# A hybrid attention block on one core: one store on another queue, one early load, two left forms behind a residual sum, and left forms taken by quarter

## The chip, the cores and the metric

The kernel runs on one core of a Trainium2 chip. Its time is the device time of one execution in microseconds (us); the figure of a kernel is the median of its runs. Beside the times there is one profiled execution, whose trace gives the start and the duration of nearly every instruction on TensorE (PE, with its weight loads as PEld), VectorE (DVE), ScalarE (ACT), GpSimd (POOL) and on SyncE's queue (SP), which issues most of the DMAs.

## The reference, cut to what matters

One layer on x of 512 rows by 2048 columns, float32:

```python
h  = rmsnorm(x, g_attn)
qa, ka, va, qb, kb, vb, f = split(h @ w_in)        # 8 + 8 heads of 128, and 8 gate columns
oa = stick_breaking_attention(qa, ka, va)          # 8 heads
ob = forgetting_attention(qb, kb, vb, cumsum(log_sigmoid(f + b_f)))   # 8 heads
x  = x + concat(headnorm(oa), headnorm(ob)) @ w_out        # w_out: 2048 x 2048
x  = x + relu(rmsnorm(x, g_mlp) @ w_up)**2 @ w_down        # 2048 x 8192, 8192 x 2048
y  = rmsnorm(x, g_final)
```

## The kernel before, in words

**Products.** Every float32 operand is split into a high part (a cast to fp32r on ACT) and a low part (what is left, a subtraction on DVE): `split`, L56 to L65. A product is three matmuls, high by high, high by low and low by high (`mm3`, L77 to L80). In a trace the three are lines L78, L79 and L80; a matmul of 128x128 by 128x512 that follows another without a wait starts 0.227 us after it. A weight tile is thus loaded as float32 by a DMA (`wraw`, `wo`, `wu`, `wd`), cast (`wh`, or `wx` where a second pair of rooms is used) and subtracted (`wl`).

**Stages.** First comes the gate and value part of the input projection, whose scaled results (`s`, scaled by the row's 1/rms) are stored to a DRAM buffer `vd` (`added`, L585 to L590: two DVE operations, then the DMA). Then follow 16 periods of 26 us, one for each head: the projections of q and k (`accq`), scores (`s`), the attention weights, and their product with v (`o`). What happens when within a period is a table of times: each job is put into a plan with `plan.at(time, job)`, and the plan is sorted by time and written out in that order (class `Plan`). In parallel the weights of the output projection are read, summed and split, and the results stored to DRAM (`wsums`, `whigh`, `wraws`). In the last period, in place of a projection, the first part of the output projection is multiplied into `acc` (class `Second`): four weight pieces of 2 x 128 rows, in the order m0 = 4, 6, 0, 2, whose high and low parts come ready from `wraws` (`load_parts`, L1142 to L1146, two DMAs each: `wh` and `wl`, for m0 = 2 both are called `w` and take rooms that held the input's left operand). At about the same time the queue issues the transposing DMA (L945, `pl<-pt`) that turns the attention weights of a head.

**The output stage** (L1490 on) computes the rest of the residual sum by a scheme of seven products instead of eight (forms p = 1 to 7; form 2 is what class `Second` multiplies; the others come in the order 1 and 4, 5, 6, 3, 7 for column half db = 0 and 1, 5, 6, 3, 7, 4 for db = 1). `g_form` makes the left operand of a form out of `mixed` (the head outputs), with at most one DVE sum or difference (`a_source`, L1335 to L1341) and a `split` (ACT cast, DVE subtraction). `out_piece(p, db, m0)` loads a weight piece and multiplies it into one of three accumulators in PSUM (`accoa`, `accob`, `accoc`). `take(p, db)` adds an accumulator to a quarter of x (DVE, L1552). When a quarter is complete, `turn_quarter` transposes it on PE in two groups of four (`tr`, L1559), ACT scales it into `hr` (L1565), SP stores it (L1574) and ACT sums its squares (L1586). Out of `hr`, `left_form` makes the seven left operands `f` of the MLP's first product, again with `a_source` and `split`. For db = 0 the quarter (0,0) is taken after the last piece of form 1, and its transposes stand after the first piece of form 5; the left operands of forms 3 and 7 are made piece by piece beside the pieces of forms 5 and 6, released by `last_heads[4]`, which is the last low part made before (L1622). `pending` lists left forms that wait for their turn in the second half.

All engines have hand-written orders: a scheduler places each instruction behind the one named in `tc.issue_after`, and each engine then runs its own list strictly in order. An instruction that waits therefore holds all that stands behind it on its engine, and this is so for SP's queue of DMAs too.

Of the kernel before, what the change touches and what calls it, by code (L numbers as in the profile page):

```python
# [12 lines left out]
ALU = mybir.AluOpType  # L13
# [25 lines left out]
def block_kernel(ctx, tc, x, g_attn, w_in, b_f, g_out_sb, g_out_fox, w_out, g_mlp, w_up, w_down, g_final, y):  # L39
    nc = tc.nc  # L40
    pe, act, dve, pool, sp = nc.tensor, nc.scalar, nc.vector, nc.gpsimd, nc.sync
# [14 lines left out]
    lows, last_heads = [None], [None] * 7  # L56
# [65 lines left out]
    vd = [dp.tile([P, TB, 2 * P], F32, name="vd0")] + [dp.tile([P, TB, 2 * NVS[i]], F32, name=f"vd{i}") for i in (1, 2)]  # L122
# [99 lines left out]
    with ExitStack() as stage:  # L222
# [23 lines left out]
        plan = Plan()  # L246
# [68 lines left out]
        t0, step = 5.9, 1.93  # L315
# [13 lines left out]
        for k in range(2, K8):  # L329
            if k < 6:  # L330
                room[k] = early_w[0][:, 4:6] if k == 2 else early_w[1][:, 2 * k - 6:2 * k - 4]
                w = Placed(room[k])
            else:
                w = Piece(w_rows[k][:, :, c0:c0 + m], 2, m)
# [41 lines left out]
        for k in range(4, K8):  # L376
            t, j = mm_at[k], k + K8
            w = pieces[k][0]
# [206 lines left out]
        def added(name, T, t0, group, j):  # L585
            out = keep[name]
            for i in range(2):
                dve.scalar_tensor_tensor(out[:, i, :], T[0][:, i, :out.shape[2]], r1s[0][:, t0 + i:t0 + i + 1], out[:, i, :], op0=ALU.mult, op1=ALU.add)
            n = NVS[group]
            sp.dma_start(vd[group][:, t0:t0 + 2, j * n:(j + 1) * n], out)  # L590

        r1s = [None]
        gate = {}
# [172 lines left out]
    with tc.tile_pool(name="att", bufs=1, side="right", reuse_waits="tile") as at, \  # L766
# [9 lines left out]
        plan = Plan()  # L776
# [403 lines left out]
        for n in range(2 * NH + 1):  # L1180
            t = TPER * n
            i_s, i_o = n - 1, n - 2
            if n < 2 * NH:
                pieces = []
                for a, (which, hf) in enumerate(((0, 0), (0, 1), (1, 0), (1, 1))):
                    if n == 0:
                        if a == 3:
                            plan.at(t + 16.3, first_pieces[a].cast)
                            plan.at(t + 18.2, first_pieces[a].low)
                        pieces.append(first_pieces[a])  # L1190
                        continue
                    load = (-21.0, -15.0, -14.0, -2.0)[a]
                    if n == 1:
                        cast, low = ((-7.0, -5.0), (-3.0, -2.0), (2.9, 3.9), (8.5, 9.5))[a]
                        load = (-23.0, -19.0, -13.1, -7.5)[a]
                    else:
                        cast, low = ((-12.35, -10.95), (2.3, 3.3), (3.9, 5.2), (9.7, 11.2))[a] if n <= NH else ((-9.25, -3.65), (2.3, 3.3), (3.3, 4.5), (13.6, 15.1))[a]
                        if a == 0 and n == NH + 1:
                            cast, low = -12.35, -10.95
                    w = q_piece(n, which, hf)  # L1200
                    if a == 3 and n > 2:
                        plan.at(t - 0.5, load_behind, w)
                        load = None
                    pieces.append(w.plan(plan, load and t + load, t + cast, t + low))
                marks = [(0, 0, 8, 0.0), (1, 0, 8, 7.35), (2, 0, 8, 14.8), (3, 0, 4, 20.3), (3, 4, 8, 23.4)]
                if n == 0:
                    marks = [(2, 0, 2, 16.2), (2, 2, 8, 17.6), (3, 0, 4, 21.6), (3, 4, 8, 24.3)]
                for a, k0, k1, dt in marks:
                    plan.at(t + dt, project, n, (0, 0, 1, 1)[a], pieces[a], a % 2, k0, k1)
                late = n <= NH  # L1210
                for which, times in ((0, (19.0, 19.75, 20.45) if n == 0 else (14.4, 18.9, 19.9) if late else (12.8, 17.9, 23.6)),
                                     (1, (TPER + 1.0, TPER + 1.7, TPER + 2.4))):
                    for dt, f in zip(times, (scale_u, high_u, low_u)):
                        plan.at(t + dt, f, n, which)
            else:
                for i, jobs in ((1, (-9.25, -3.65)), (0, (2.3, 3.3))):
                    for dt, f in zip(jobs, (fox_left.high, fox_left.low)):
                        plan.at(t + dt, f, i)
                unit = 0
                for db in range(2):  # L1220
                    for n0, m0 in enumerate((4, 6, 0, 2)):
                        w = Second(db, m0)
                        if db:
                            plan.at(t + (-10.0, -9.0, -8.0, 6.0)[n0], w.load)
                            plan.at(t + (3.4, 4.5, 10.3, 11.35)[n0], w.cast_apart if n0 < 2 else w.cast, *((n0,) if n0 < 2 else ()))
                            plan.at(t + (4.6, 7.0, 11.75, 12.95)[n0], w.low)
                        else:
                            plan.at(t + (-11.0, -5.5, 0.1, 0.2)[n0], w.load_parts)
                        for tt in range(2):
                            plan.at(t + at_unit16(unit), w.multiply, tt)  # L1230
                            unit += 1
                for db in range(2):
                    plan.at(t + 2.0 + db, load_second_x, db)
                    for tt in range(2):
                        plan.at(t + (20.6, 28.5)[db] + 0.75 * tt, take_second, db, tt)
                t_end = t + at_unit16(15) + 1.37
# [31 lines left out]
        t = TPER * 2 * NH  # L1268
# [229 lines left out]
    def g_form(p, *parts):  # L1498
        for m0, m1 in parts:
            a_form(p, mixed_halves[:, m0:m1], [g[:, m0:m1, :] for g in G[p]])  # L1500
# [35 lines left out]
            begun_ = sp.dma_start(raw, wsums[:, m0 // 2, {5: 0, 7: 1, 4: 2, 6: 3}[p], db])  # L1536
        return raw, begun_

    units, casts = [], [None]
    first_loads = [(u, k, slice(a, a + 2)) for u in range(2) for k in range(2) for a in range(0, KC // 2, 2)]  # L1540
    hr, quarter = [[None, None], [None, None]], {}

# [4 lines left out]
    def take(p, db):  # L1547
        qs, ps = {1: ([(0, 0)], chains[db]), 5: ([(1, 1)], C), 6: ([(0, 1)], chains[db]),
                  7: ([(1, 1), (1, 0)], chains[db]), 3: ([(0, 1)], C), 4: ([(1, 0)], (early_4, C)[db])}[p]
        for q in qs:  # L1550
            for t in range(2) if p == 4 else [slice(0, 2)]:
                dve.tensor_tensor(quarter[q][:, t, :], quarter[q][:, t, :], ps[:, t, :], op=ALU.add)  # L1552

    def turn_group(t0, j, db, a):
        x_ = quarter[t0, j]
# [35 lines left out]
        a_form(p, hr[db][j], [F[p][db][:, 2 * j:2 * j + 2, c, :] for c in range(2)])  # L1591

    pending, to_turn = [], []
    for db in range(2):
        quarter[0, 0] = second_x[db]
        if db == 1:
            pending += [(1, 0, j) for j in (1, 0)]
        else:

            g_form(1, (0, 4), (4, 6))  # L1600
            with tc.issue_after(last_heads[2].ins):
                g_form(4, (0, 4), (4, 8))
            with tc.issue_after(last_heads[5].ins):
                g_form(5, (0, 4), (4, 6))
            more_parts.append(lambda: parts_at(px, "px"))
            with tc.issue_after(last_heads[3].ins):
                out_piece(1, 0, 0)
            with tc.issue_after(last_heads[0].ins):
                out_piece(1, 0, 2)
                out_piece(1, 0, 4)  # L1610
            begin(1, 0, 0)
            with tc.issue_after(last_heads[1].ins):
                for m0 in (0, 2, 4, 6):
                    ins = out_piece(4, 0, m0)
            for p in (1, 5):
                g_form(p, (6, 7), (7, 8))
            take(4, 0)
            with tc.issue_after(ins.ins):
                begin(1, 1, 0)
            with tc.issue_after(last_heads[6].ins):  # L1620
                g_form(6, (0, 4), (4, 6), (6, 8))
            last_heads[4] = lows[0]  # L1622
        for p in (1, 5, 6, 3, 7, 4)[:6 if db else 5]:
            for m0 in (6,) if db == 0 and p == 1 else (0, 2, 4, 6):
                ins = out_piece(p, db, m0)
                if m0 in (0, 2) and to_turn:
                    with tc.issue_after(ins.ins):
# [16 lines left out]
                if db == 0 and p == 5 and m0 == 6:  # L1644

                    with tc.issue_after(ins.ins):
                        begin(0, 1, db)
                if db == 0 and p in (6, 5) and m0 != 0:

                    with tc.issue_after(last_heads[4].ins):  # L1650
                        g_form({5: 3, 6: 7}[p], {2: (0, 4), 4: (4, 6), 6: (6, 8)}[m0])
            if db == 0 and p == 6:
                more_parts.pop()
                px_cm.__exit__(None, None, None)
# [5 lines left out]
                begin(1, 1, db)  # L1660
            if db == 1 and p == 3:
                begin(1, 0, db)
            take(p, db)
            if db == 1:
                pending += [(q, 0, j) for q in {1: (4, 5, 6), 6: (2, 7, 3)}.get(p, ()) for j in range(2)]
            if len(squares) > 0:

                with ExitStack() as order_:
                    if casts[0] is not None:
                        order_.enter_context(tc.issue_after(casts[0].ins))  # L1670
                    take_squares()
            to_turn += [q + (db,) for q in {1: [(0, 0)], 3: [(0, 1)], 7: [(1, 1)] if db else [(1, 1), (1, 0)]}.get(p, ())]
            if db == 1 and p == 6:
                left_form(1, 1, 0)
        if db == 1:
# [167 lines left out]
    plan, groups = Plan(), {}  # L1843
# [9 lines left out]
    for u, p, begin_, total, cast, low in (  # L1853
# [3 lines left out]
        w = FirstProduct(u, p)  # L1857
# [4 lines left out]
    for p, j, total, cast, low in ((7, 1, None, -1.0, 1.5), (4, 0, None, 5.95, 7.1), (5, 0, 7.8, 8.45, 9.7), (6, 0, 14.1, 14.85, 16.0),  # L1862
                                   (7, 0, 16.7, 17.45, 18.6), (3, 1, 24.2, 25.5, 26.35), (3, 0, 27.0, 28.4, 28.5)):
        w = Left(p, j)
# [85 lines left out]
    with tc.manual_schedule(engines={pe.engine, act.engine, dve.engine}):  # L1950
# [7 lines left out]
        for k in range(len(steps)):  # L1958
            n = steps[k][2]
# [6 lines left out]
            w, p = at_step(k - 1)  # L1966
# [298 lines left out]
```

## Time and profile before

| what | value |
|---|---|
| median of 3 runs | 2015.63 us (2014.76 to 2016.26) |
| the profiled execution | 2014.26 us |
| its span, first to last instruction | 2012.5 us |
| granted TensorE clock, mean over the span | 0.998 |
| PE busy | 1992.4 us (99%) |
| DVE busy | 1754.9 us (87%) |
| ACT busy | 1205.4 us (60%) |
| data moved by DMA | 426.66 MB, 212 GB/s on average |

The profiled execution is 1.37 us faster than the median, and 1.8 us of it lie outside the span. Views of the trace give, for an instruction or a run of equal ones, the start in us from the span's start, the duration, the engine and line, the operation with its output and inputs, and in brackets the idle time of the engine just before it and what ended that. A list of waits adds such idle times up by what was waited for. Lines are those of the kernel before.

### The profile page before, as it was taken

The page shows a single profiled execution, that of the slowest core. Times are in us where ns is not written, and L with a number is a line of the kernel's source. Part 1 is how long each engine was busy: PE and PEld are TensorE (multiplying, and loading weights), DVE is VectorE, ACT ScalarE, POOL GpSimd, SP SyncE. Part 2 cuts the span into 40 slices and gives each one's busy share as a digit, 9 for nine tenths or more (in the row PEclk, how much of TensorE's full clock was granted, in tenths as well). Part 3 has the DMA queues.
Part 4 walks back from the last instruction along what each step waited for, and adds up shares of the span by engine and source line. Part 5 has one row for each costly group of instructions (what it writes and reads, how often), then busy time and mean ns, then how long its engine had stood idle before and what let it go on. Part 6 is the DMA issues. An engine that isn't in the chain of part 4 may idle for free.

```text
span 2012.5 us, 26673 instructions
## 1 busy us (share of the span) xinstructions
PE 1992.4 (99%) x10096; PEld 1710.1 (85%) x10096; DVE 1754.9 (87%) x1992; ACT 1205.4 (60%) x1636; POOL 64.8 (3%) x73
## 2 busy tenths in 40 slices
PE   9999999999999999999999999999999999999998
PEld 9988788888887889888888888888888888888887
DVE  7876788888888579999999999998798888888896
ACT  7543567778875466776676767766543444444444
POOL 0000011101110000000000000000000000000003
PEclk9999999999999999999999999999999999999999
DMA  7335877677797872566666675666794674674642
GB/s 259 126 141 178 285 252 233 200 226 216 225 286 249 261 259 99 166 209 214 201 197 204 197 223 187 206 203 233 251 330 175 228 269 162 232 266 167 217 164 84
DMA packets 309072, 426.66 MB, mean 212 GB/s; under 512 B 49440, under 2 KB 198736, under 8 KB 302416
## 3 DMA queue, kind: packets, MB, share of 16 engines
q1 hardware_dynamic: 308192, 422.85, 63.5%
q10 hardware_dynamic: 752, 2.11, 0.3%
q8 instruction: 79, 1.29, 0.2%
q14 instruction: 49, 0.40, 0.1%
HBM read 318.07 MB, written 97.01 MB: 206 GB/s over the span
## 4 chain that ended last, share of the span: by engine, by line
PE 95%; DMA 2%; DVE 2%; ACT 1%; issue 0%; SPq 0%; DVEq 0%; ACTq 0%
PE psa L1415 11%; PE accd L80 8%; PE accd L78 8%; PE accd L79 8%; PE psa L1413 6%; PE psc L1415 5%; PE accq L78 5%; PE accq L79 5%; PE accq L80 5%; PE psc L1413 3%; PE psb L1415 3%; PE psb L1413 1%; PE m L80 1%; PE m L79 1%; PE m L78 1%; PE vy L78 1%
## 5 line engine op out<-in xcount | busy, mean ns | idle before, releaser
L2051 ACT CAST wh<-wd 128x1024 fp32r<-128x1024 f32 x126 | 125.0, 998 | 167.4 <-PE accd L80 55.9
L1937 DVE TENSOR_TENSOR wl<-wu,wh 128x1024 fp32r<-128x1024 f32 x157 | 191.4, 1220 | 13.4 <-ACT wh L1931 13.4
L80 PE MATMUL accq<-hH,wl 128*128 128x512 f32 x512 | 199.5, 390 | 1.1 <-DVE wl L180 1.1
L78 PE MATMUL accq<-hH,wh 128*128 128x512 f32 x512 | 200.4, 391 | 0.0
L79 PE MATMUL accq<-hL,wh 128*128 128x512 f32 x512 | 199.4, 389 | 0.0
L1931 ACT CAST wh<-wu 128x1024 fp32r<-128x1024 f32 x157 | 166.4, 1060 | 48.5 <-PE psc L1415 22.9
L1415 PE MATMUL psa<-f,wh 128*128 128x512 f32 x712 | 177.1, 391 | 0.0
L79 PE MATMUL accd<-wl,uf 128*128 128x512 f32 x436 | 169.6, 389 | 0.0
L80 PE MATMUL accd<-wh,uf 128*128 128x512 f32 x436 | 169.6, 389 | 0.0
L78 PE MATMUL accd<-wh,uf 128*128 128x512 f32 x436 | 169.4, 389 | 0.0
L2058 DVE TENSOR_TENSOR wl<-wd,wh 128x1024 fp32r<-128x1024 f32 x126 | 144.0, 1152 | 11.5 <-ACT wh L2051 11.5
L1415 PEld LDWEIGHTS psa<-f,wh 128*128 128x128 f32 x712 | 130.8, 188 | 25.3
L2051 ACT CAST wx<-wd 128x1024 fp32r<-128x1024 f32 (+1 forms) x82 | 80.8, 995 | 107.9 <-PE accd L80 43.2
L1772 DVE TENSOR_TENSOR m<-m,accd 128x1024 f32<-128x1024 f32 x84 | 102.3, 1217 | 48.5 <-PE accd L80 48.5
L80 PEld LDWEIGHTS accq<-hH,wl 128*128 128x128 f32 x512 | 96.1, 188 | 21.9 <-DVE wl L180 1.6
L79 PEld LDWEIGHTS accq<-hL,wh 128*128 128x128 f32 x512 | 96.2, 188 | 18.9
L78 PEld LDWEIGHTS accq<-hH,wh 128*128 128x128 f32 x512 | 96.2, 188 | 18.9
L78 PE MATMUL accd<-wx,uf 128*128 128x512 f32 x284 | 110.5, 389 | 0.0
L79 PE MATMUL accd<-wx,uf 128*128 128x512 f32 x284 | 110.5, 389 | 0.0
L80 PE MATMUL accd<-wx,uf 128*128 128x512 f32 x284 | 110.5, 389 | 0.0
L1413 PEld LDWEIGHTS psa<-f,wl 128*128 128x128 f32 x712 | 94.8, 191 | 5.2
L1413 PE MATMUL psa<-f,wl 128*128 128x256 f32 x712 | 97.2, 282 | 0.0
(498 smaller groups left out, 5073.8 us busy)
## 6 DMA issues: line engine op xcount, KB each, us to landing
wu<-in_w_up_dram SPq DMA_DIRECT2D x60, 1024.0 KB, 6.6
ufd<-st SPq DMA_DIRECT2D x98, 512.0 KB, 3.6
wd<-in_w_down_dram SPq DMA_DIRECT2D x48, 1024.0 KB, 8.4
uf<-ufd SPq DMA_DIRECT2D x42, 1024.0 KB, 7.0
wraw<-in_w_in_dram SPq DMA_DIRECT2D x64, 512.0 KB, 5.8
wo<-wsums SPq DMA_DIRECT2D x28, 512.0 KB, 5.3
wd<-in_w_down_dram SPq DMA_DIRECT2D x16, 768.0 KB, 8.3
uf<-ufd SPq DMA_DIRECT2D x14, 768.0 KB, 4.5
```

Of the source, the lines that this page charges most:

```text
L78: pe.matmul(out, sh, mh, start=first, stop=False, skip_group_check=True)
L79: pe.matmul(out, sh, ml, start=False, stop=False, skip_group_check=True)
L80: return pe.matmul(out, sl, mh, start=False, stop=last, skip_group_check=True)
L1413: ins = pe.matmul(ps[:, 2 * P:], lo[:, a, :], f_parts(p, a)[0], start=False, stop=last, skip_group_check=True)
L1415: ins = pe.matmul(ps, hi[:, a, :], f_both(p, a), start=a == PAIRS[0] and p in (1, 5), stop=last, skip_group_check=True)
L1772: dve.tensor_tensor(M[p][:, :, db, :], M[p][:, :, db, :], ps, op=ALU.add)
L1931: act.copy(rooms[k][0], srcs[k])
L1937: lows[0] = dve.tensor_tensor(lo, srcs.pop(k), hi.bitcast(F32), op=ALU.subtract)
L2051: act.copy(rooms[k + 3][0], srcs[k + 3])
L2058: dve.tensor_tensor(rooms[k + 2][1], srcs.pop(k + 2), rooms[k + 2][0].bitcast(F32), op=ALU.subtract)
```

## The change

Six places change.

1. The last store of scaled values (group 2, name "21") is issued by ACT's queue, the others stay on SP's.
2. The parts of the piece m0 = 2, the fourth of `Second`, are loaded by the plan at t - 1.4 instead of t + 0.2; the transposing DMA of the head before stands at t - 1.25 and the piece m0 = 0 at t + 0.1.
3. The left operands of forms 3 and 7 are made later: a table `G_AT` says beside which piece (p, m0) which parts are made, and they are released by the residual sum of quarter (0,0) (`taken[0]`), not by the last low part before.
4. For db = 0 the last piece of form 1, the sum of quarter (0,0) (`take(1, 0)`) and the entry of its transposes into `to_turn` move from ahead of form 5 to ahead of form 5's last piece; the transposes come after the first piece of form 6.
5. With that, `take` and `to_turn` skip form 1 of db = 0 at their old place.
6. In `pending`, left forms of db = 1 are listed quarter by quarter (j outer, form q inner) instead of form by form.

```diff
@@ added
-            sp.dma_start(vd[group][:, t0:t0 + 2, j * n:(j + 1) * n], out)
+            (act if group == 2 and name == "21" else sp).dma_start(vd[group][:, t0:t0 + 2, j * n:(j + 1) * n], out)
@@ the plan of the last period
-                            plan.at(t + (-11.0, -5.5, 0.1, 0.2)[n0], w.load_parts)
+                            plan.at(t + (-11.0, -5.5, 0.1, -1.4)[n0], w.load_parts)
@@ take
-                dve.tensor_tensor(quarter[q][:, t, :], quarter[q][:, t, :], ps[:, t, :], op=ALU.add)
+                taken[0] = dve.tensor_tensor(quarter[q][:, t, :], quarter[q][:, t, :], ps[:, t, :], op=ALU.add)
@@ output stage
+    G_AT = {(5, 6): (3, (0, 4), (4, 6)), (6, 0): (3, (6, 8)), (6, 2): (7, (0, 4)), (6, 4): (7, (4, 6)), (6, 6): (7, (6, 8))}
...
-            last_heads[4] = lows[0]
         for p in (1, 5, 6, 3, 7, 4)[:6 if db else 5]:
-            for m0 in (6,) if db == 0 and p == 1 else (0, 2, 4, 6):
+            for m0 in () if db == 0 and p == 1 else (0, 2, 4, 6):
+                if db == 0 and p == 5 and m0 == 6:
+                    out_piece(1, 0, 6)
+                    take(1, 0)
+                    last_heads[4] = taken[0]
+                    to_turn += [(0, 0, 0)]
                 ins = out_piece(p, db, m0)
...
-                if db == 0 and p in (6, 5) and m0 != 0:
+                if db == 0 and (p, m0) in G_AT:
 
                     with tc.issue_after(last_heads[4].ins):
-                        g_form({5: 3, 6: 7}[p], {2: (0, 4), 4: (4, 6), 6: (6, 8)}[m0])
+                        g_form(*G_AT[p, m0])
...
-            take(p, db)
+            if db == 1 or p != 1:
+                take(p, db)
             if db == 1:
-                pending += [(q, 0, j) for q in {1: (4, 5, 6), 6: (2, 7, 3)}.get(p, ()) for j in range(2)]
+                pending += [(q, 0, j) for j in range(2) for q in {1: (4, 5, 6), 6: (2, 7, 3)}.get(p, ())]
...
-            to_turn += [q + (db,) for q in {1: [(0, 0)], 3: [(0, 1)], 7: [(1, 1)] if db else [(1, 1), (1, 0)]}.get(p, ())]
+            to_turn += [q + (db,) for q in {1: [(0, 0)] if db else [], 3: [(0, 1)], 7: [(1, 1)] if db else [(1, 1), (1, 0)]}.get(p, ())]
```

The first place is the end of the value part (about 175 to 195 us of the trace). ACT's order there, with - for rows of before alone and + for rows of the changed kernel alone; `wh<-wraw` are casts of projection weights of the first head, `vd` is the DRAM buffer of values:

```order
 L173 CAST wh<-q_1573 128x1024
 L173 CAST wh<-r_1593 128x1024
-L173 CAST wh<-wraw 128x1024 x3
+L173 CAST wh<-wraw 128x1024 x2
+L590 DMA vd_89<-s_1700 128x2x512
+L173 CAST wh<-wraw 128x1024
 L801 CAST uh<-qf 128x512
 L173 CAST wh<-wraw 128x1024
```

The store stands between the second and the third cast; on SP's queue its row is gone from between a load of `wraw` and the load of `rb` (L784), and nothing else moves there.

The second place is SP's queue at the start of the last period (about 581 to 596 us). `wh` and `wl` are the parts of the pieces m0 = 6 and then m0 = 0, `w` with a number those of the piece m0 = 2, and the transposing DMA is that of the head before:

```order
 L1146 DMA wh<-wraws_94 128x1024
 L1146 DMA wl<-wraws_94 128x1024
+L1146 DMA w_5249<-wraws_94 128x1024
+L1146 DMA w_5248<-wraws_94 128x1024
 L1146 DMA wh<-wraws_94 128x1024
+L945 DMA_TRANSPOSE pl<-pt 128x20x128
 L1146 DMA wl<-wraws_94 128x1024
-L1146 DMA w_5264<-wraws_94 128x1024
-L945 DMA_TRANSPOSE pl<-pt 128x20x128
-L1146 DMA w_5265<-wraws_94 128x1024
 L166 DMA wraw<-in_w_out_dram 128x2x512
 L1536 DMA wo<-wsums 128x1024
```

Both parts of m0 = 2 now stand ahead of the transposing DMA, and the low part of m0 = 0 stands behind it, where before the second part of m0 = 2 stood. Three loads are ahead of the transposing DMA in both orders.

The third place is DVE's order around the sum of quarter (0,0) (about 646 to 663 us). The rows L1341 and L1339 are the differences for the left operands of forms 3 and 7, `g` their low parts, `x<-x,accoa` the sum of quarter (0,0), and `x<-x,accoc` that of form 5's quarter:

```order
 L61 TENSOR_TENSOR g_5518<-mixed,g_5517 128x512
+L1552 TENSOR_TENSOR x_5278<-x_5278,accoa 128x1024
 L1341 TENSOR_TENSOR mixed<-mixed 128x4x256
 L1341 TENSOR_TENSOR mixed<-mixed 128x2x256 x2
 L1339 TENSOR_TENSOR mixed<-mixed 128x4x256
 L1339 TENSOR_TENSOR mixed<-mixed 128x2x256 x2
-L1552 TENSOR_TENSOR x_5278<-x_5278,accoa 128x1024
-L61 TENSOR_TENSOR wx<-wo,wx 128x1024
+L1552 TENSOR_TENSOR x_5703<-x_5703,accoc 128x1024
 L61 TENSOR_TENSOR g_5522<-mixed,g_5521 128x1024
```

The sum of quarter (0,0) moves ahead of the six differences, and the low part of a weight piece (`wx`) leaves its place behind it, since that piece is loaded earlier. On PE the transposes `tr` of this quarter move from ahead of the first piece of form 6 to behind it. In the second half of the stage the two transpose groups of one quarter, which stood 12 matmuls apart, now stand one right behind the other, and on DVE the difference `hr` for a left operand of form 7 (L1339) now stands ahead of a weight's low part (`wl<-wu,wh`, L1838) instead of behind it.

More of the change, by code (lines that the diff above doesn't have):

```diff
@@ L1537, in out_weights @@
         return raw, begun_
-    units, casts = [], [None]
+    units, casts, taken = [], [None], [None]
     first_loads = [(u, k, slice(a, a + 2)) for u in range(2) for k in range(2) for a in range(0, KC // 2, 2)]
```

## The prediction

> **What bounds the kernel now.** I read the page first, then PE's list of waits, then the timeline around each wait. The page's row for PE (busy us, share of the span, instructions):
>
> ```profile
> PE 1992.4 (99%) x10096; PEld 1710.1 (85%) x10096; DVE 1754.9 (87%) x1992; ACT 1205.4 (60%) x1636; POOL 64.8 (3%) x73
> ```
>
> PE is busy for 1992.4 of 2012.5 us, and the change alters no matmul, only orders. So all that it can take away is idle PE time, and all that it can cost is new idle time. PE's waits (us in total, times, longest):
>
> ```profile
> PE tr L1559 <- DVE x L1552: 4.3, 1, 4.3
> PE acc L79 <- DMA w<-wraws: 2.0, 1, 2.0
> PE vx L306 <- DVE still L302: 1.6, 1, 1.6
> PE s L78 <- ACT uk L801: 1.3, 1, 1.3
> PE o L79 <- DVE pl L956: 1.1, 1, 1.1
> PE accq L80 <- DVE wl L180: 1.1, 1, 1.1
> PE tr L1559 <- ACT hr L1565: 0.8, 1, 0.8
> PE accoc L78 <- ACT wx L60: 0.5, 1, 0.5
> PE s L79 <- DVE uk L805: 0.2, 1, 0.2
> ```
>
> That is 12.9 us in nine waits. The 1.6 us stand at the start, where nothing changes. The others fall into the places that the change touches: A, the first head's periods (1.1 + 1.3 + 0.2 + 1.1 = 3.7); B, the last period (2.0); C, the residual sum (4.3 + 0.5); D, the end of the output stage (0.8).
>
> **A, the store on ACT's queue.** SP's queue, ACT, DVE and PE around the store, from the timeline (start, duration, in brackets the idle time before and what ended it):
>
> ```profile
> 174.91 0.46 SPq L166 DMA_DIRECT2D wraw<-in_w_in_dram  x1
> 185.59 0.37 SPq L590 DMA_DIRECT2D vd<-s  x1
> 186.05 0.42 SPq L784 DMA_DIRECT2D rb<-r1d  x1
> 186.52 4.43 SPq L166 DMA_DIRECT2D wraw<-in_w_in_dram  x3
> ```
>
> ```profile
> 184.15 1.41 DVE L588 SCALAR_TENSOR_TENSOR s<-vz,r1v,s 128x512 f32<-128x512 f32 x2 [0.86 <-PE vz L80]
> 192.64 1.05 ACT L173 CAST wh<-wraw 128x1024 fp32r<-128x1024 f32 x1 [10.61 <-DMA wraw<-in_w_in_dram]
> 196.12 0.50 PE L80 MATMUL accq<-hH,wl 128*128 128x512 f32 x1 [1.13 <-DVE wl L180]
> ```
>
> SP's queue issues nothing from 175.4 to 185.59, because the store waits for the DVE operations that end at 185.56. Behind it stand `rb` and three weight loads; ACT then idles 10.6 us for a weight, and PE at last 1.13 us for that weight's low part. The windows (length, busy us of PE, PEld, DVE, ACT, POOL, granted clock, DMA share, GB/s) show the backlog:
>
> ```profile
> 175.00:191.00 16.00, 16.00 (x73) 13.23 (x72) 6.22 (x6) 4.75 (x6) 0.00 (x0) 1.00 0.48 133
> 191.00:236.00 45.00, 41.24 (x185) 33.37 (x184) 30.80 (x48) 22.53 (x30) 2.56 (x4) 1.00 0.91 292
> ```
>
> The DMA engines were half idle while the queue stood, and PE's four waits of A all lie in the stretch after, with the DMAs at 0.91. With the store on ACT, SP can issue `rb` and the loads up to 10 us earlier. On ACT the store holds what stands behind it until 185.56: the third cast (192.64 before) and the score casts, none of which had run earlier, so this is free; the added issue costs ACT about the 0.37 us that it took SP. Each wait costs PE some 0.16 us more than its idle time, as the restart in B's rows shows (2.37 us from start to start, less a step of 0.23, for 1.98 of idle). If all four go: 3.7 + 4 x 0.16 = 4.4 us. Bounds: the first wait alone (-1.1), and all of it with slow restarts (-4.8); a loss is excluded unless ACT is late, and it idles there. I take -4.4: the first wait has 7 us of room, and the later three hang on ACT and DVE work fed by that backlog.
>
> The Trainium skill, page "DMA: Bandwidth & Descriptors", section "Issuing engines are not separate DMA queues", says that issuing from several engines saves only the sequencer's time to start a DMA. By that rule A would be worth about the 0.37 us of the issue. The row at 185.59 speaks against it: what is saved is the issuing engine's wait, not its issue. It is a rival below.
>
> **B, the fourth early piece.** SP's queue and all transposing DMAs (duration ns min, median, max):
>
> ```profile
> 588.52 6.66 SPq L945 DMA_TRANSPOSE pl<-pt  x1
> 595.24 0.57 SPq L1146 DMA_DIRECT2D w<-wraws  x1
> L945 SPq DMA_TRANSPOSE pl<-pt x15: 2425/2557/6664, 222.4 to 588.5; - x15
> ```
>
> ```profile
> 594.40 0.39 PE L79 MATMUL acc<-wl,g 128*128 128x512 f32 x1
> ...
> 596.90 0.39 PE L78 MATMUL acc<-w,g 128*128 128x512 f32 x1
> 599.27 0.50 PE L79 MATMUL acc<-w,g 128*128 128x512 f32 x1 [1.98 <-DMA w<-wraws]
> ```
>
> This transposing DMA holds the queue for 6.66 us where the median is 2.56. It has three fresh loads ahead of it; that it waits for them is my reading. The load behind it is issued at 595.24 and releases PE at 599.27, 4.03 us later. The new order puts the second part of m0 = 2 ahead, as it says, but the low part of m0 = 0 behind. Three loads are still ahead, so I expect the queue held as long and the load behind to land at the same time. Yet PE needs the low part of m0 = 0 at 594.40, eleven matmuls and 2.50 us before the first one of m0 = 2 (0.227 us each). So PE would stand from the end of the matmul ahead of it, 594.57 at the latest, until 599.27, and the twelve matmuls that it did before in that time follow after: 596.90 + 0.23 - 594.40 = +2.7 us net (the old wait goes, one of some 4.7 us of idle comes).
>
> A stall that long has a second price, seen in C: after 4.26 us of idle the granted clock fell to 0.83 in the window, and 1.5 us more were lost (worked out there); after the 1.98 us here it stayed at 1.00:
>
> ```profile
> 590.00:600.00 10.00, 8.02 (x39) 6.51 (x38) 6.74 (x8) 7.17 (x7) 0.76 (x1) 1.00 1.04 262
> 650.00:660.00 10.00, 5.93 (x25) 5.18 (x26) 9.83 (x12) 7.26 (x15) 0.00 (x0) 0.83 0.80 297
> ```
>
> An idle stretch of 4.7 us is nearest to the 4.26, so I add 1.5: B = +4.2. Bounds: -2.1 (the queue comes free early and the wait vanishes) and +5 (the low part lands a little later).
>
> The Trainium skill, page "TensorE: Matmul & The Clock Gate", section "What's actually happening", says that the clock halves after an idle window of about 3.4 us, and that these windows run free of the kernel. By that rule a stall of 4.7 us would hold a whole window in only about 4 in 10 of its placings ((4.7 - 3.4)/3.4, an estimate), and B would come to about +3.3 on average. The 4.26 us that dropped and the 1.98 us that didn't agree with it and can't settle it.
>
> **C, the sum of quarter (0,0).** DVE, then PE:
>
> ```profile
> 647.51 0.69 DVE L61 TENSOR_TENSOR g<-mixed,g 128x512 fp32r<-128x512 f32 x1 [0.69 <-ACT g L60]
> 648.12 2.42 DVE L1341 TENSOR_TENSOR mixed<-mixed 128x1024 f32<-128x1024 f32 x3
> 650.46 2.42 DVE L1339 TENSOR_TENSOR mixed<-mixed 128x1024 f32<-128x1024 f32 x3
> 652.80 1.22 DVE L1552 TENSOR_TENSOR x<-x,accoa 128x1024 f32<-128x1024 f32 x1
> ```
>
> ```profile
> 649.30 0.50 PE L78 MATMUL accoc<-wx,g 128*128 128x512 f32 x1 [0.46 <-ACT wx L60]
> 654.07 1.97 PE L1559 MATMUL tr<-ident,x 128*128 128x128 f32 x8 [4.26 <-DVE x L1552]
> 655.69 0.78 PE L78 MATMUL accoa<-wh,g 128*128 128x512 f32 x1
> ...
> 657.00 0.40 PE L78 MATMUL accoa<-wh,g 128*128 128x512 f32 x1
> ```
>
> The same eight transposes where nothing held PE up before them:
>
> ```profile
> 686.26 1.04 PE L1559 MATMUL tr<-ident,x 128*128 128x128 f32 x8
> ```
>
> The sum stands behind six differences for forms 3 and 7 (4.7 us), and the transposes stand at PE's front. The cost now: 654.07 - 649.30 - 0.23 = 4.5 for the transposes' wait; 0.46 + 0.16 = 0.6 for the weight `wx`; then the slow clock: 1.97 - 1.04 = 0.9 in the transposes and 1.31 - 0.68 = 0.6 in three matmuls. Together 6.6 us, of which 1.5 is clock.
>
> After the change the sum stands ahead of the differences, and on PE one piece of 12 matmuls (2.7 us) lies between the accumulator's last matmul and the transposes. The sum needs 1.22 us behind at most one other operation (0.69 us, with 0.69 of idle ahead of it): 2.6 of 2.7 us, so I leave 0.5 for it. Next late would be form 6's weights, loaded from `whigh`:
>
> ```profile
> wh<-whigh SPq DMA_DIRECT2D x3, 512.0 KB, 8.4
> ```
>
> They take 8.4 us to land (median), and PE now comes to them 5 us sooner; for that I leave 0.5, up to 3. The left operands of forms 3 and 7 are needed a whole form later (four pieces of 2.7 us). C = -6.6 + 1.0 = -5.6, between -6.6 and -3.1.
>
> **D, left forms by quarter.** The trace shows one wait here, 0.8 for `tr`: the transposes wait for ACT to read an older group. The second group now stands right behind the first, without 12 matmuls between, and should wait once more as long: +0.8. On DVE two operations of 0.69 us move ahead of low parts of weights that PE needs at the start of the MLP (1.4); half of it should show: +0.6. D = +1.4, between 0 and +3; the front-loading of a whole quarter's forms could also remove the 0.8, but no row says so.
>
> **Sum.** -4.4 + 4.2 - 5.6 + 1.4 = -4.4 us. The profiled execution (2014.26) would become 2009.9; the median stands 1.4 above it, and 2015.63 - 4.4 = 2011.2 us. A change of 0.2%, 4.0 us, is about what a measurement of this kernel can tell from none, so the forecast lies just beyond it.
>
> **Rivals.** R1: DVE, not the order, is the bound at C; it is busy for 9.83 of 10 us in 650:660, so PE's gain comes back as waits for low parts: C = 0, sum +1.2, 2016.8. Against it stands the next stretch, where DVE has room:
>
> ```profile
> 660.00:680.00 20.00, 20.00 (x90) 16.57 (x89) 9.42 (x8) 5.62 (x6) 0.00 (x0) 1.00 0.67 212
> ```
>
> R2: the store's new queue saves only its issue, since the loads behind are held by their rooms anyway: A = -0.4, sum -0.4, 2015.2. R3: nothing takes the place of the removed waits. The transposing DMA lets the queue go after its median 2.56 us, some 4 us sooner, and B is near 0; C = -6.1, D = 0: sum -10.5, 2005.1. For it: only one of the long holds is seen with three loads ahead. R4, slower: at D the left operands, now by quarter, come too late for the MLP's first products. Each missing one costs about three operations of 0.69 us in series (difference, cast, low part; for the cast an estimate), 2.1 us; six of them are 12.6 instead of 1.4, and the sum is +6.8, 2022.4. It decides against the change from the fifth missing operand on (4.4 + 4.0 = 8.4 more than forecast, so D of 9.8). Against it: only 0.8 us of wait in this stretch now.
>
> **Chances.** The forecast's case 0.52 (own range -7.5 to -1; faster by over 0.2% in 0.32, within in 0.20), R1 0.14, R2 0.14 (both within 0.2%), R3 0.12 (faster), R4 0.08 (slower). So faster 0.44, same 0.48, slower 0.08. The range reaches from -8.4 (the forecast's case with B at its lower price and a part of what lies between it and R3) to +1.4 (R1 and R2 whole): 2007.2 to 2017.0; left out are R4 and the rest of R3.
>
> **What would show it.** A: no wait of PE between 190 and 240 us, no standstill on SP's queue from 175 to 185. B: a wait of `acc` L79 on `wl<-wraws` of 4 to 5 us in place of 2.0 on `w`, and a granted clock below 1 in its window. C: the wait of `tr` on L1552 at 0.5 or less, clock 1.00. D: a second wait of `tr` on L1565. The prediction is wrong if B's wait is gone or under 1 us, if waits on `wh<-whigh` exceed 3 us, if A's four waits remain, or if PE waits over 5 us past 735 us.

## The result, and the profile after

The changed kernel takes 2011.54 us in the median of 13 runs, against 2015.63 of before in the same job; the ratio is 0.9978 (95% interval 0.9969 to 0.9987). That is 4.1 us, just past the 0.2% that the prediction named as the limit of what can be told. The forecast was 2011.2. One of the 13 runs took 4343.0 us, which nothing here explains, and the ratio leaves it out. The profiled execution of the changed kernel took 2010.09 us (before 2014.26), its span is 2008.3 us.

PE's list of waits after (us in total, times, longest):

```profile
PE acc L79 <- DMA wl<-wraws: 3.7, 1, 3.7
PE vx L306 <- DVE still L302: 1.6, 1, 1.6
PE accoa L78 <- DMA wh<-whigh: 0.9, 1, 0.9
PE acc L78 <- ACT w L873: 0.8, 1, 0.8
PE psc L79 <- DVE f L1828: 0.7, 1, 0.7
PE psb L80 <- DVE wl L1844: 0.4, 1, 0.4
PE tr L1559 <- DVE x L1552: 0.3, 1, 0.3
PE accoc L79 <- DVE wl L61: 0.3, 1, 0.3
PE tr L1559 <- ACT hr L1565: 0.3, 1, 0.3
```

The four waits of A are gone, that of 4.3 us at C is 0.3, the 2.0 on `w` became 3.7 on `wl`, and five small ones are new. To see what each place was worth, follow the same four instructions through both traces: the first matmul of `Second`, its first in the second row half of m0 = 2, the transposes of the next quarter, and the first matmul of the MLP. Before:

```profile
586.91 0.39 PE L78 MATMUL acc<-wh,g2h 128*128 128x512 f32 x1
601.90 0.39 PE L78 MATMUL acc<-w,g2h 128*128 128x512 f32 x1
...
763.47 0.28 PE L78 MATMUL psa<-f,wh 128*128 128x256 f32 x1
```

and after:

```profile
581.35 0.39 PE L78 MATMUL acc<-wh,g2h 128*128 128x512 f32 x1
600.60 0.39 PE L78 MATMUL acc<-w,g2h 128*128 128x512 f32 x1
680.70 1.03 PE L1559 MATMUL tr<-ident,x 128*128 128x128 f32 x8
757.42 0.28 PE L78 MATMUL psa<-f,wh 128*128 128x256 f32 x1
```

The third stood at 686.26 before. After minus before is -5.56, -1.30, -5.56, -6.05 and at the end of the span -4.2. Of the first, 0.52 were there ahead of the change (the DVE operations of the last store start at 183.63 instead of 184.15). So:

| place | forecast | measured between equal instructions |
|---|---|---|
| A, the store | -4.4 | -5.0 |
| B, the early piece | +4.2 | +4.3 |
| C, the residual sum | -5.6 | -4.3 |
| D, to the first MLP matmul, and behind it | +1.4 | -0.5 and +1.9 |
| ahead of A | 0 | -0.5 |
| sum | -4.4 | -4.2 (in the medians -4.1) |

A after, on SP's queue and on ACT:

```profile
174.38 0.46 SPq L166 DMA_DIRECT2D wraw<-in_w_in_dram  x1
174.94 0.92 SPq L784 DMA_DIRECT2D rb<-r1d  x1
175.91 7.26 SPq L166 DMA_DIRECT2D wraw<-in_w_in_dram  x3
```

```profile
185.08 0.40 ACTq L590 DMA_DIRECT2D vd<-s  x1
185.60 1.05 ACT L173 CAST wh<-wraw 128x1024 fp32r<-128x1024 f32 x1 [4.08 <-DVE s L588]
```

`rb` is loaded 11 us sooner, and the third cast, held behind the store on ACT as foretold, starts at 185.60 where it started at 192.64.

B after, on SP's queue and on PE, with a window (length, busy us of PE, PEld, DVE, ACT, POOL, granted clock, DMA share, GB/s):

```profile
582.95 6.72 SPq L945 DMA_TRANSPOSE pl<-pt  x1
589.72 0.57 SPq L1146 DMA_DIRECT2D wl<-wraws  x1
```

```profile
589.53 0.47 PE L78 MATMUL acc<-wh,g 128*128 128x512 f32 x1 [0.75 <-ACT w L873]
593.67 0.64 PE L79 MATMUL acc<-wl,g 128*128 128x512 f32 x1 [3.67 <-DMA wl<-wraws]
...
597.09 0.49 PE L78 MATMUL acc<-wh,g 128*128 128x512 f32 x1
```

```profile
590.00:600.00 10.00, 6.33 (x22) 5.10 (x22) 6.48 (x7) 7.86 (x7) 1.69 (x2) 0.83 0.68 203
```

The transposing DMA holds the queue for 6.72 us, the low part behind it releases PE 3.95 us after its issue, and from 593.67 to 597.09 eight matmuls start 0.427 us apart instead of 0.227: the clock is halved for 3.4 us and 1.6 us are lost.

C after, on DVE and PE:

```profile
649.23 1.21 DVE L1552 TENSOR_TENSOR x<-x,accoa 128x1024 f32<-128x1024 f32 x1
650.36 2.42 DVE L1341 TENSOR_TENSOR mixed<-mixed 128x1024 f32<-128x1024 f32 x3
```

```profile
650.50 1.09 PE L1559 MATMUL tr<-ident,x 128*128 128x128 f32 x8 [0.32 <-DVE x L1552]
...
655.25 0.50 PE L78 MATMUL accoa<-wh,g 128*128 128x512 f32 x1 [0.91 <-DMA wh<-whigh]
...
661.52 0.50 PE L79 MATMUL accoc<-wl,g 128*128 128x512 f32 x1 [0.31 <-DVE wl L61]
```

The sum runs ahead of the differences, the transposes take 1.09 us instead of 1.97, and two small waits follow.

### The profile page after: what moved, and what is told of

Same layout as the page of the kernel before. It is cut to its first block, busy times and chain, and to the rows that moved or that the text cites. A ratio compares the mean times of both kernels' runs of the same rounds, so it can differ in the third digit from the quotient of the medians.

```text
span 2008.3 us, 26668 instructions
## 1 busy us (share of the span) xinstructions
PE 1992.1 (99%) x10096; PEld 1709.8 (85%) x10096; DVE 1754.1 (87%) x1992; ACT 1204.9 (60%) x1636; POOL 63.4 (3%) x73
## 3 DMA queue, kind: packets, MB, share of 16 engines
q10 hardware_dynamic: 1024, 2.63, 0.3%
## 4 chain that ended last, share of the span: by engine, by line
PE 95%; DVE 2%; DMA 1%; ACT 1%; issue 0%; DVEq 0%; SPq 0%; ACTq 0%
PE psa L1415 11%; PE accd L80 8%; PE accd L78 8%; PE accd L79 8%; PE accq L78 6%; PE accq L80 6%; PE accq L79 6%; PE psa L1413 6%; PE psc L1415 5%; PE psc L1413 3%; PE psb L1415 3%; PE psb L1413 1%; PE m L80 1%; PE m L78 1%; PE m L79 1%; PE vy L79 1%
```

## The experiments

The letters are those of the prediction. All times are medians beside the kernel before in the same job. A change in us that stands behind a ratio is the ratio applied to the time of before; it can differ by up to 1 us from the difference of the two medians.

### Each part alone

Four kernels take one part each into the kernel before: `a_only` the first line of the diff, `b_only` the second, `c_only` the parts three to five (shown with the change), `d_only` the last.

```diff
 a_only
-            sp.dma_start(vd[group]..., out)
+            (act if group == 2 and name == "21" else sp).dma_start(vd[group]..., out)
 b_only
-  (-11.0, -5.5, 0.1, 0.2)[n0]
+  (-11.0, -5.5, 0.1, -1.4)[n0]
 d_only
-  for q in {1: (4, 5, 6), 6: (2, 7, 3)}.get(p, ()) for j in range(2)
+  for j in range(2) for q in {1: (4, 5, 6), 6: (2, 7, 3)}.get(p, ())
```

> The kernel before with the first part alone: the last store of values on ACT's queue. Theory: the queue's standstill from 175.4 to 185.59 us is the cause of PE's four waits between 196 and 236 us, so all four go and the time falls by 4.4 us as forecast (5.0 us as the trace of the changed kernel reads it between equal matmuls). Rival R2: only the issue of 0.4 us is saved, and the time is within 0.5 us of before. A second rival: the later three waits come from the load of the DMAs themselves, then only the first goes, 1.3 us.

Measured: 2010.24 against 2015.93, ratio 0.9974 (0.9965 to 0.9983), that is -5.2 us (-3.4 to -7.1). PE's whole list of waits:

```profile
PE tr L1559 <- DVE x L1552: 4.1, 1, 4.1
PE acc L79 <- DMA w<-wraws: 2.9, 1, 2.9
PE vx L306 <- DVE still L302: 1.6, 1, 1.6
PE tr L1559 <- ACT hr L1565: 0.9, 1, 0.9
PE accoc L78 <- ACT wx L60: 0.5, 1, 0.5
```

No wait of A is left, so all four hung on the queue's standstill; R2 is out, and so is the milder rival. By R2's rule, that issuing from another engine saves only the issue, this kernel would have gained 0.4 us. The Trainium skill states this rule on the page "DMA: Bandwidth & Descriptors", section "Issuing engines are not separate DMA queues"; the measurement decides against it here: what the store blocked was a queue of other loads, by its wait of 10 us, and the issue of 0.4 us hardly counts.

> The kernel before with the second part alone: the fourth piece's parts at t - 1.4. Theory: the transposing DMA still holds the queue until the three loads ahead have landed, the low part of m0 = 0 lands as late as the second part of m0 = 2 did, PE idles 3.7 to 4.7 us there instead of 2.0, the clock halves for about 3.4 us, and the time rises by 4.2 us. Rival: the stall is an effect of the other parts (loads that moved forward, ACT late at the attention weights), and alone this part costs at most 1 us or gains up to 2.

Measured: 2018.78 against 2015.93, ratio 1.0019 (1.0010 to 1.0028), +3.8 us (+2.0 to +5.6). PE waits 3.77 us on `wl<-wraws`, and the matmuls behind it start 0.43 us apart: the clock halves. The part costs what the theory says, alone too.

> The kernel before with the residual sum of quarter (0,0) ahead and the left operands of forms 3 and 7 later, nothing else. Theory: the wait of 4.3 us and the slow clock behind it go, waits of 0.3 on the sum and about 0.9 on form 6's weights come, and the time falls by 4.3 us. Rival R1 (DVE is the bound there): PE's gain comes back as waits for low parts before 680 us, and the time falls by under 1 us.

Measured: 2010.87 against 2015.93, ratio 0.9975 (0.9965 to 0.9986), -5.0 us (-2.8 to -7.1); PE waits 1.0 us on the sum and 0.8 on `whigh`. R1 is out: no wait for a weight's low part comes behind it, so DVE had room.

> The kernel before with the left forms of the second half by quarter, nothing else. Theory: the time rises by 1.4 us, from waits at the start of the MLP on DVE's low parts and left operands (psb and psc). Rival: these waits come from PE's being earlier by the other parts, and alone this part costs nothing or gains 0.5 us (the transposes' wait falls from 0.8 to 0.3).

Measured: 2016.19 against 2015.93, ratio 1.0001 (0.9992 to 1.0009). The rival holds: alone this part costs nothing that can be told. So the +1.4 of the changed kernel needs something else as well.

### The parts together, and the transposing DMA

`ac` takes A and C into the kernel before; `ac_all_ahead` and `ac_all_behind` then place all four loads of m0 = 0 and m0 = 2 ahead of the transposing DMA, or behind it:

```diff
 ac_all_ahead
-  (-11.0, -5.5, 0.1, 0.2)[n0]
+  (-11.0, -5.5, -1.5, -1.4)[n0]
 ac_all_behind, in load_parts
+                    if self.m0 in (0, 2):
+                        with tc.issue_after(now["turn"].ins):
+                            sp.dma_start(w.bitcast(F32), wraws[1][:, self.m0 // 2, i])
```

> The kernel before with the store on ACT and the residual sum ahead; the early piece and the left forms stay as before. Theory (the parts add up): -5.2 and -5.0 as measured alone, so about -10 us against before, near 2006. Rival: the gains share something (with PE earlier by 5 us the loads of the output stage are late), and the two together give at most -7.

Measured: 2006.9 against 2014.26, ratio 0.9959 (0.9945 to 0.9973), -8.3 us (-5.4 to -11.1). The single gains add to 10.2, inside the interval, but it doesn't exclude the rival's 7 either.

> As the kernel with the store and the sum changed, and the parts of both m0 = 0 and m0 = 2 planned ahead of the transposing DMA (t - 1.5 and t - 1.4), so that four loads stand ahead of it and none behind. Theory: PE needs no load behind the transposing DMA any more, the wait of 2 to 3 us on w goes, and the time falls by 2 us more, to about 2004; the transposing DMA holds the queue for one load longer, 7.5 to 8.5 us. Rival: the loads behind it (residual weights of the output stage) or the transposed weights come later by that 1.3 us and a new wait eats the gain: same as without, 2006.

Measured: 2007.04, ratio 0.9960 (0.9947 to 0.9973): no gain over `ac` in the median. The wait on `w` is gone as expected, and a new one stands behind, at 603.41, on the product that uses the transposed weights:

```profile
PE o L79 <- DVE pl L956: 1.4, 1, 1.4
```

The transposing DMA held the queue for 6.89 us; 7.5 to 8.5 were expected, and with three loads ahead it takes 6.21 to 7.84 in the traces here. The profiled execution (2004.11) is the fastest of the five; whether this order gains on `ac` isn't settled.

> As the kernel with the store and the sum changed, and all four loads of m0 = 0 and m0 = 2 placed behind the transposing DMA on SP's queue. This tells whether its long hold comes from the loads ahead of it. Theory: with no fresh load ahead it holds the queue for 2.4 to 2.7 us, as the others do, the four loads follow at once, and PE waits once on m0 = 0's parts. Rival: it holds the queue for over 6 us whatever stands ahead (its own data come late), and PE waits 5 us or more for m0 = 0.

Measured: 2005.2, ratio 0.9951 (0.9937 to 0.9966), -9.9 us (-6.9 to -12.7). SP's queue:

```profile
583.20 2.59 SPq L945 DMA_TRANSPOSE pl<-pt  x1
585.88 0.53 SPq L1148 DMA_DIRECT2D wh<-wraws  x1
```

With no fresh load ahead the transposing DMA holds the queue for 2.59 us. So its long hold comes from the loads ahead of it, which the prediction had only read from the rows. That it lasts until they have landed fits the one landing that the trace of before gives: the load of `wl` issued at 587.29 took 8.1 us and landed at 595.4, and the queue was free at 595.18. The four loads behind the transposing DMA cost PE two waits, 0.6 and 0.7 us, where one was expected, and no slow clock.

### Where D's cost comes from

> The changed kernel with the left forms listed form by form again; everything else is changed. Theory after the run of that part alone (which cost nothing): the waits at the start of the MLP in the changed kernel (0.4 on psb, 0.7 on psc) come from this order only when PE is early, and go with it: -1.4 us against the changed kernel, 2010. Rival: they come from PE's being 5 us earlier whatever the order, and the time stays at 2011.5.

Measured: 2010.35 against 2014.26, ratio 0.9980 (0.9971 to 0.9989): not to be told from the changed kernel's 0.9978 by the times. By the traces, from the first MLP matmul to the end of the span this kernel takes 1249.3 us (2011.0 less 761.68), the changed one 1250.9 (2008.3 less 757.42), before 1249.0. The stretch speaks for the theory, the times leave it open. In the profiled execution, the slowest of this kernel's eleven, 14 matmuls ran at half clock behind the wait on `wl`, against 8 in the changed kernel's, which hides a gain of this size.

DVE's order then shows a difference between the changed kernel and `d_only`: two rows at the start of the MLP are swapped. In the changed kernel the left operand's low part (`f`) stands ahead of the weight's (`wl`). ACT's order has the same swap: the cast of that `f` stands ahead of the weight's cast (`wh`). DVE, then ACT:

```profile
764.32 0.68 DVE L1337 TENSOR_TENSOR hr<-hr 128x512 f32<-128x512 f32 x1
765.69 0.69 DVE L61 TENSOR_TENSOR f<-hr,f 128x512 fp32r<-128x512 f32 x1 [0.69 <-ACT f L60]
766.90 1.23 DVE L1844 TENSOR_TENSOR wl<-wu,wh 128x1024 fp32r<-128x1024 f32 x1 [0.52 <-ACT wh L1841]
```

```profile
765.03 0.62 ACT L60 CAST f<-hr 128x512 fp32r<-128x512 f32 x1 [3.45 <-DVE hr L1337]
765.83 2.00 ACT L1841 CAST wh<-wu 128x1024 fp32r<-128x1024 f32 x2
```

ACT idles 3.45 us for DVE's L1337 and only then casts the weight; on DVE `f` waits for its cast, and `wl` stands behind `f` and waits for the late `wh` as well. Two kernels tell the swap from the other parts, since the scheduler happens to swap in one and not in the other: `no_b` (the changed kernel with -1.4 back at 0.2; not swapped) and `a_and_d` (the first and the last line of the diff alone; swapped).

> The changed kernel with the early piece back at t + 0.2; the other parts stay. Here DVE's order at the start of the MLP has a weight's low part (wl<-wu) ahead of a left operand's (f<-hr), as in the kernel with the left forms alone; in the changed kernel the two are swapped. Theory: the early piece costs 4 us, and the left forms by quarter cost 1.4 us only through that swap; both go, the time is 5 to 6 us below the changed kernel, near 2006, and from the first MLP matmul to the end the trace takes 1249.0 to 1249.5 us. Rival: the left forms by quarter cost this whenever PE is early, whatever the swap; the time is 4 us below, near 2007.5, and that stretch takes 1250.9 us as in the changed kernel.

Measured: 2006.68 against 2015.96, ratio 0.9953 (0.9941 to 0.9966), -9.5 us. The stretch takes 1249.5 us (2005.0 less 755.46). The same three operations there:

```profile
762.35 0.68 DVE L1337 TENSOR_TENSOR hr<-hr 128x512 f32<-128x512 f32 x1
762.95 1.22 DVE L1844 TENSOR_TENSOR wl<-wu,wh 128x1024 fp32r<-128x1024 f32 x1
764.09 0.68 DVE L61 TENSOR_TENSOR f<-hr,f 128x512 fp32r<-128x512 f32 x1
```

`wl` follows at once, and DVE doesn't idle. On ACT the cast of this weight had started at 759.78, ahead of that of `f` at 763.07.

> The kernel before with the store on ACT and the left forms by quarter, no other part. Here DVE's order has the swap (left operand's low part ahead of the weight's). Theory: the stretch from the first MLP matmul to the end takes 1250.5 to 1251 us as in the changed kernel, against 1249.0 in every kernel without the left forms by quarter, and the time is 1.4 us over that of the store alone. Rival: the cost needs the residual sum's new place (PE early at the output stage, DVE's order there), and the stretch takes 1249.0 to 1249.5 us.

Measured: 2012.29 against 2015.96, ratio 0.9982 (0.9973 to 0.9992). That is 1.6 us above the store alone (0.9974), near the 1.4 of the theory, but the two intervals overlap. The stretch takes 1250.9 us (2010.2 less 759.31), with the waits of the changed kernel:

```profile
PE psc L79 <- DVE f L1822: 0.7, 1, 0.7
...
PE psb L80 <- DVE wl L1838: 0.4, 1, 0.4
```

So the cost comes with the swap and without C, and it doesn't come with C and without the swap. From the first MLP matmul on, the orders of PE, DVE, ACT and SP's queue differ between `d_only` and `a_and_d` in the place of this one `f` alone (its cast on ACT, its low part on DVE), and so they do between `no_b` and the changed kernel. The stretch takes 1249.0 to 1249.3 us in the eight kernels with the forms in the old order, 1249.5 in the three by quarter without the swap (`d_only`, `no_b`, `lows_last`), and 1250.9 in the two with it. The left forms by quarter thus cost 1.9 us at the MLP in orders with the swap, and 0.5 in those without.

### Needing the late low part later

`lows_last` is the changed kernel, but m0 = 0 multiplies its high part first for both row blocks, and its low part last:

```diff
+                if self.m0 == 0 and self.db == 0:
+                    for i in range(2):
+                        for g in (gh, gl):
+                            pe.matmul(second_ps[0][t], g[:, i, ts], self.hi[:, i, :], ...)
+                    for t_ in range(2) if t else ():
+                        for i in range(2):
+                            pe.matmul(second_ps[0][t_], gh[:, i, ...], self.lo[:, i, :], ...)
```

> The changed kernel, but the piece m0 = 0 of the last period multiplies its high part first for both row blocks (8 matmuls) and its low part last (4 matmuls), so that PE needs the low part behind the transposing DMA 7 matmuls, 1.6 us, later. DVE's order at the start of the MLP has no swap here. Theory: the wait on wl<-wraws falls from 3.7 to about 2.1 us; the half clock behind it (1.6 us) goes unless the idle time falls into one stretch as in the kernel with the left forms alone; with the swap gone too (1.4) the time falls by 3 to 4.6 us, to 2007 to 2008.5. Rival: the wait isn't set by when the low part lands (ACT's or another load's lateness holds PE), and stays above 3 us.

Measured: 2006.66 against 2015.96, ratio 0.9953 (0.9940 to 0.9965), -9.5 us, some 5 us under the changed kernel's ratio. Of these, 1.4 us belong to the swap, which this order doesn't have (its stretch takes 1249.5 us). PE:

```profile
589.88 2.06 PE L1161 MATMUL acc<-wh,g 128*128 128x512 f32 x8 [0.64 <-DMA wh<-wraws]
594.26 1.20 PE L1164 MATMUL acc<-wl,g 128*128 128x512 f32 x4 [2.32 <-DMA wl<-wraws]
```

The wait falls from 3.67 to 2.32 us and the clock stays full: four matmuls in 1.04 us (the next starts at 595.30). The landing of the low part sets the wait.

## Why the prediction was right, point by point

**A** was right in cause and a little small: -4.4 forecast, -5.0 in the trace and -5.2 (-3.4 to -7.1) alone. The doubt about the three later waits was needless; all four went.

**B** was right in sum, and its parts moved against each other. The reading that the queue is held by the loads ahead (6.72 us as before, 2.59 without them), and that the low part of m0 = 0 comes as late as `w` did, held; +4.2 was forecast, +4.3 came. But PE idled 3.67 us there and not 4.7 (the sign named was 4 to 5), because it came to that matmul later: 0.75 us of wait stand one matmul ahead of it, which weren't forecast. The list puts them down to ACT; in `b_only`, `no_d` and `lows_last` the same matmul waits 0.66, 0.84 and 0.64 us for the DMA of m0 = 0's high part, `wh`. That load now stands third in the row ahead of the transposing DMA, so it is the likelier cause in the changed kernel too, though its trace doesn't name it. The slow clock was 1.6 us, not 1.5. That the sum came out within 0.1 is in part luck.

**C** was right in cause, and its remaining waits were mis-sized: "I leave 0.5" for the sum and "0.5, up to 3" for `whigh` make 1.0, where the trace loses 0.5 on the sum, 1.1 on `whigh` and 0.5 on a weight's low part on DVE, counted from start to start less a step; the last was on no list of the prediction. The slow clock that went was 1.4 us by the same count, not 1.5: the eight transposes took 1.62 us to the next start where they take 0.85 after the change. The measured -4.3 lies inside the bounds given (-6.6 to -3.1).

**D** came out at the number forecast, +1.4, by another way, so this step failed and the number was luck. "The second group should wait once more as long" is wrong: the wait of `tr` on L1565 fell from 0.8 to 0.3, and no second one came. And the late low parts at the MLP cost 1.9 instead of 0.6, not through two operations moved ahead but through one left operand whose cast on ACT and low part on DVE moved ahead of a weight's. Edits elsewhere bring that swap about or undo it (it is there in `a_and_d` and the changed kernel, not in `d_only`, `no_b` and `lows_last`); why the scheduler swaps isn't shown. The prediction looked at DVE's order there and didn't follow which row waits for ACT.

**The sum** of -4.4 lies near the measured -4.2 partly by errors that cancel: C gained 1.3 us less than forecast, A 0.6 more, and 0.5 were gained ahead of A, where nothing was changed.

**The rivals.** R1, R2 and R4 are out: A and C gained alone, and nothing past 735 us waited over 0.7 us. R3's premise was wrong in the changed kernel, and right where the loads stand behind the transposing DMA. The Trainium skill's free-running window (page "TensorE: Matmul & The Clock Gate", section "What's actually happening") would have given B about +3.3 on average, by the prediction's estimate. The clock did halve at 3.67 us of idle here, and behind all seven other waits in these traces that were longer; the rows were the better guide to this term.

Three kernels beat the changed one by about 5 us, with intervals that don't touch its own: `no_b` (0.9953), `lows_last` (0.9953) and `ac_all_behind` (0.9951). They can't be told apart.

## What to carry to other kernels

A DMA that waits on a queue costs what stands behind it, not its own issue (here 5.2 us against 0.4): ask which load is next in that queue and who idles for it, and move the waiting DMA to an engine that idles anyway. When a load is moved ahead of something slow, look which load takes its old place, and when its first reader comes: here one moved ahead of a transposing DMA pushed one behind it that was needed 2.5 us sooner. And where a scheduler orders the engines, parts that are free alone can cost together, through an order that no line of the diff shows.

## What the runs showed of the hardware that was not expected

The transposing DMA on SP's queue holds it longer when loads were issued shortly ahead: 6.2 to 7.8 us with three fresh loads of 512 KB ahead (eleven traces), 6.9 with four, 2.59 with none (one trace each). The first transposing DMA of the kernel before, at 222.44 us, has two other transfers 0.8 and 1.2 us ahead and holds it for 5.07.

The clock can halve after far less idle time than the 4.26 us of before. In `d_only`:

```profile
598.38 0.50 PE L79 MATMUL acc<-w,g 128*128 128x512 f32 x1 [1.82 <-DMA w<-wraws]
598.71 0.39 PE L80 MATMUL acc<-w,g 128*128 128x512 f32 x1
598.94 0.55 PE L78 MATMUL acc<-w,g 128*128 128x512 f32 x1
599.29 0.63 PE L79 MATMUL acc<-w,g 128*128 128x512 f32 x1
599.72 0.63 PE L80 MATMUL acc<-w,g 128*128 128x512 f32 x1
```

After 1.82 us of idle PE runs on at full clock for half a microsecond (steps of 0.23 us), then at half (0.43). In the traces here the clock halved at 1.82 and 2.63 us (`no_b`) and at every wait of 3.67 us or more, and it stayed at 1.93, 1.98, 2.23, 2.32, 2.48 and 2.92 us (the last in `a_only`). The length alone doesn't decide at 2 to 3 us; that the drop comes late, and not with the idle time, fits a window that runs free of the kernel, as the Trainium skill says (page "TensorE: Matmul & The Clock Gate", section "What's actually happening"). It doesn't fit the figure given there, that the clock halves after at least one idle window of about 3.4 us: 1.82 us were enough.
